# Inverse square roots as one GpSimd power, and filling products ahead of the first scores of an attention

## The chip, the cores and the metric

One NeuronCore of a Trainium2 chip runs the whole program. The metric is the device time of one execution in microseconds (us), as the median of several runs. The core's engines are TensorE (PE, with PEld for its weight loads), VectorE (DVE), ScalarE (ACT), GpSimd (POOL) and SyncE (SP, which only issues DMAs). Each engine works through its own instructions in order; semaphores make one wait for another.

## The reference

The program is a two-layer encoder over 512 tokens of width 1024. The first layer has two attentions side by side, A (grouped queries, normalised per head) and B (through latents), the second layer a neighbourhood attention; each layer ends in an MLP, and a last norm closes. What matters here is where an inverse square root is taken: in every RMS norm, of tokens, of heads and of latents.

```python
def rmsnorm(x, g):
    xf = x.astype(jnp.float32)
    y = xf * lax.rsqrt(jnp.mean(xf * xf, axis=-1, keepdims=True) + EPS)
    return (y * g.astype(jnp.float32)).astype(x.dtype)
...
    z = h @ w_in
    qa, ka, va, cq, ckv, kr = jnp.split(z, EVEN_SPLITS, axis=-1)
    qa = axial_rope(rmsnorm(qa.reshape(b, s, A_HEADS, HEAD_DIM), a_q_norm), row, col)
    ka = axial_rope(rmsnorm(ka.reshape(b, s, A_KV_HEADS, HEAD_DIM), a_k_norm), row, col)
    va = va.reshape(b, s, A_KV_HEADS, HEAD_DIM)
    oa = block_attention(qa, ka, va, HEAD_DIM ** -0.5)
    qb = (rmsnorm(cq, b_q_norm) @ b_w_uq).reshape(b, s, B_HEADS, B_NOPE + B_ROPE)
    ...
    kvb = (rmsnorm(ckv, b_kv_norm) @ b_w_ukv).reshape(b, s, B_HEADS, B_NOPE + B_V)
```

## The kernel before

**Precision.** Matrix products run on values split into a high and a low part (`hi`, `lo`): the high part is a rounded copy made by ACT, the low part the difference made by DVE or POOL. A product of two split operands is three matmuls (L501 to L503 for the dense ones).

**The first layer's beginning.** The input x is transposed to feature-major tiles, and the first 768 columns of the input projection (one key tile, one value tile, four query tiles of A) are accumulated in six PSUM banks. While the last products run, the banks are emptied one after the other. First comes the token norm: `compact_r` (L522, L524) sums the squares and makes `r0`, [128, 4], through `rsqrt`, and L764 and L765 copy and square it. Then the key tile: `stat` squares it and reduces per head by matmuls (L593 ACT, L594 DVE, L595 POOL, L596 and L597 PE), `stats_to_tok` turns the result token-major (L572 ACT, L575 PE), scales it by `r0sq` (L578), adds epsilon (L580) and takes the root `rsA`, [128, 8] (L582). L661 spreads it, PE's L530 transposes it back, L665 multiplies the rotated key, and L669 and L670 split it. After that the four query tiles pass through the same `stat`, and `q_scales` makes their root `rsQ`, [128, 32], and from it `scA` (L710). `rope_q(0)` rotates the first query tile (L560 DVE, L562 POOL, L563 and L566 DVE) and splits it (L623 ACT, L624 DVE); the three other tiles come later, through DMAs (`far`).

**The attention.** `attend` (L961) walks over 64 steps: 32 for A (8 heads of four 128-query blocks), then 32 for B. A step makes its scores (L997, two matmuls of 512 columns in A, three in B) into one of two score banks `s`; DVE's L1001 scales them, takes the extreme and moves them out of the bank, in A with `scA` as the scale; ACT's L1003 takes the exponential; DVE's L1004 and POOL's L1005 normalise. Three steps later PE transposes the probabilities (L972, four matmuls), ACT and DVE split them (L974, L975), and every second step the value products follow (L985, eight matmuls); after four steps a head is folded (L946 ACT, L949 DVE).

**The fillers.** Between these, `step` calls `fill.run(1.5)`: it takes products from a queue for as many microseconds as a credit says, each product with a nominal price (`MM3`, 0.69 for three matmuls). In the queue are the rest of the input projection (L501 to L503, split by ACT's L212 and DVE's or POOL's L202), the rotary key, the latents (whose norm takes the root `rsB`, [128, 8]) and B's first projections of queries, keys and values (L907 to L909 for the values); from step 35 on, the output projection and the second half of B's projections. `heads_B` empties the queue before it begins.

**The order.** Here nothing is fixed by hand: the code gives the order in which the operations are written, and a scheduler moves instructions of one engine past each other where data allow. So neither the written place of `rsqrt` nor that of the fillers is the place that they get. Only in the second layer's attention is the written order kept (`fixed_order`).

**The root.** `rsqrt` is used seven times: for r0, rsA, rsQ and rsB in the first layer, once in each MLP (L1136 broadcasts it), and for the second attention's tokens (L1313). `rsqrt_steps` (L155) makes a first guess from the bits of the number (L159, L160), halves and negates the number (L162), and does three Newton steps of three operations (L166, L167, L169): twelve DVE instructions on a tile of 4, 8 or 32 columns. `soon` would put a step off where the order is fixed by hand; `rsqrt` is not called there.

Of the kernel before, what the change touches and what calls it, by code (L numbers as in the profile page):

```python
# [8 lines left out]
F32 = mybir.dt.float32  # L9
F32R = mybir.dt.float32r  # L10
I32 = mybir.dt.int32
AF = mybir.ActivationFunctionType
ALU = mybir.AluOpType
# [5 lines left out]
P = 128  # L19
# [11 lines left out]
def f32(ap):  # L31
    return ap.bitcast(F32)
# [3 lines left out]
def encoder_kernel(ctx: ExitStack, tc: tile.TileContext, ins, out, dbg=None):  # L36
    nc = tc.nc
    PE, ACT, DVE, POOL, SP = nc.tensor, nc.scalar, nc.vector, nc.gpsimd, nc.sync
# [22 lines left out]
    def nm(s):  # L61
        cnt[0] += 1
        return f"{s}_{cnt[0]}"
# [18 lines left out]
    def sbk():  # L82
        return bank("s", 2)

    def stb():
        return bank("t", 2)

    def ob():
        return bank("o", 1)
# [4 lines left out]
    def tiny(n, dt=F32):  # L94
        return tp.tile([P, n], dt, tag=f"ti{n}", name=nm("ti"))

    def keep(shape, dt, name):
        return big.tile(shape, dt, tag=name, name=name)
# [8 lines left out]
    POOL.memset(ones, 1.0)  # L107
    zeros = keep([P, 1], F32, "zeros")
    POOL.memset(zeros, 0.0)
    gs = Slot(F32)  # L110
    ACT.dma_start(cst, ins["cst"][:, 0:C_ROPE])
    ACT.dma_start(gs.t[0:16, 0:P], ins["norm_mix"].rearrange("l (k p) -> (l k) p", p=P))
# [42 lines left out]
    def rsqrt_steps(v, n, then):  # L155

        y = tiny(n)
        yi = y.bitcast(I32)
        DVE.tensor_scalar(yi, v.bitcast(I32), 1, None, op0=ALU.logical_shift_right)  # L159
        DVE.tensor_scalar(yi, yi, -1, 0x5F3759DF, op0=ALU.mult, op1=ALU.add)  # L160
        hv = tiny(n)
        DVE.tensor_scalar(hv, v, -0.5, 1.0, op0=ALU.mult, op1=ALU.mult)  # L162

        def newton(y, left):
            a = tiny(n)
            DVE.tensor_tensor(a, y, y, op=ALU.mult)  # L166
            DVE.tensor_tensor(a, a, hv, op=ALU.mult)  # L167
            y2 = tiny(n)
            DVE.scalar_tensor_tensor(y2, a, 1.5, y, op0=ALU.add, op1=ALU.mult)  # L169
            if left:  # L170
                soon(lambda: newton(y2, left - 1))
            else:
                then(y2)

        newton(y, 2)

    def rsqrt(v, n):
        got = []
        rsqrt_steps(v, n, got.append)
        return got[0]  # L180
# [83 lines left out]
    def soon(z, later=None):  # L264
        if fixed[0]:
            (off_d if later is None else later).append(z)
        else:
            z()
# [202 lines left out]
    class Fill:  # L471
# [8 lines left out]
        def step(self):  # L480
            try:
                self.credit -= next(self.q[0][1])
            except StopIteration:
                self.q.pop(0)
# [13 lines left out]
    fill = Fill()  # L498
# [442 lines left out]
    def fold(o, e):  # L941

        if e == 0:
            hold["pair"] = scratch()
        a, c, pair = 64 * e, scratch(), hold["pair"]
        ACT.activation(c[0:64, :], o[64:128, :], AF.Copy)  # L946

        def add():
            DVE.tensor_tensor(pair[a : a + 64, :], o[0:64, :], c[0:64, :], op=ALU.add)  # L949
            if e:  # L950
                O.append(Slot())
                soon_a(lambda o=O[-1]: split(pair, o.pair()))

        soon(add)
# [6 lines left out]
    def attend(heads, step):  # L961


        late_t, late_v = [], []

        def transpose(h, i, p):
            if i % 2 == 0:
                h["pt"] = Slot(), Slot()
            h3, l3 = (s_.t.rearrange("p (k q) -> p k q", k=4)[:, :, (i % 2) * P : (i % 2 + 1) * P] for s_ in h["pt"])
            tb = stb()  # L970
            for k in range(4):
                PE.transpose(tb[:, k * P : (k + 1) * P], p[:, k * P : (k + 1) * P], ident)  # L972
            t3 = tb.rearrange("p (k q) -> p k q", k=4)
            ACT.activation(h3, t3, AF.Copy)  # L974
            DVE.tensor_tensor(l3, t3, f32(h3), op=ALU.subtract)  # L975
            if i % 2:
                late_v.append((h, i // 2, h["pt"]))

        def values(h, half, pt):
            if half == 0:  # L980
                h["o"] = ob()
            o = h["o"]
            for k in range(4):
                for n, m in enumerate(pt):
                    PE.matmul(o[:, 256 * half : 256 * half + 256], h["vlhs"](k), m.t[:, 256 * k : 256 * k + 256],  # L985
                              start=k == 0 and n == 0, stop=k == 3 and n == 1, skip_group_check=True)
            for s_ in pt:
                s_.free()
            if half:
                fold(o, h["e"])  # L990
                h["after"]()

        def scores(h, i):
            s = sbk()
            pl = h["passes"](i)
            for n, (lh, rh) in enumerate(pl):
                PE.matmul(s, lh, rh, start=n == 0, stop=n == len(pl) - 1)  # L997
            h["done"](i)
            t = tiny(4)
            p = pp.tile([P, 512], F32, tag="p", name=nm("p"))  # L1000
            DVE.tensor_tensor_reduce(p, s, zeros.to_broadcast([P, S]), op0=ALU.add, op1=ALU.min, scale=h["scale"](i),  # L1001
                                     scalar=3e38, accum_out=t[:, 1:2])
            ACT.activation(p, p, AF.Exp, bias=t[:, 1:2], scale=-1.0, accum_out=t[:, 2:3])  # L1003
            DVE.reciprocal(t[:, 3:4], t[:, 2:3])  # L1004
            POOL.tensor_scalar(p, p, t[:, 3:4], 1.0, op0=ALU.mult, op1=ALU.mult)  # L1005
            return p

        for h in heads:
            for i in range(4):
                ripe = list(late_v)  # L1010
                p = scores(h, i)
                if len(late_t) == 3:
                    transpose(*late_t.pop(0))
                late_t.append((h, i, p))
                if ripe:
                    values(*late_v.pop(0))
                step(h, i)
        for x in late_t:
            transpose(*x)
            while late_v:  # L1020
                values(*late_v.pop(0))
            fill.run(1.5)

    def heads_A():
        for h in range(8):
            t, e, kv = h // 2, h % 2, h // 4
            if e == 0 and t < 3:
                rope_q(t + 1)
            q, k = QA[t].pair(), KA[kv].pair()

            def done(i, t=t, e=e):
                if e == 1 and t < 3 and i == 0:
                    sum_q(t + 1)
                if i == 3 and e:
                    QA[t].free()
                    if t % 2:
                        KA[t // 2].free()

            yield dict(e=e, done=done, scale=lambda i, h=h: hold["scA"][:, i, h : h + 1],
                       passes=lambda i, q=q, k=k, e=e: [(q[:, e, i * P : (i + 1) * P], k[:, z, :]) for z in range(2)],  # L1040
                       vlhs=lambda kt, kv=kv: VAv[:, kt, kv, :], after=VA.free if h == 7 else lambda: None)

    def heads_B(g):
        fill.until(f"v{g}")
        Q, K, V = (QKV[g][z] for z in "QKV")
        vv = [s_.t.rearrange("p (i h e) -> p i h e", i=2, h=4) for s_ in V]
        for j in range(4):
            q, k = Q[j].pair(), K[j].pair()

            def passes(i, q=q, k=k):  # L1050
                ts = slice(i * P, (i + 1) * P)
                return [(q[0:96, 0, ts], k[0:96, 0, :]), (q[0:96, 1, ts], k[0:96, 0, :]),
                        (q[0:96, 0, ts], k[0:96, 1, :])]

            def done(i, j=j):
                if i == 3:
                    Q[j].free()
                    K[j].free()

            def after(j=j):  # L1060
                if j == 3:
                    for s_ in V:
                        s_.free()

            yield dict(e=j % 2, done=done, after=after, scale=lambda i: hold["scB"][:, i : i + 1], passes=passes,
                       vlhs=lambda kt, j=j: vv[kt // 2][:, kt % 2, j, :])
# [3 lines left out]
    def all_heads():  # L1070
        yield from heads_A()
        yield from heads_B(0)
        yield from heads_B(1)
# [18 lines left out]
    fill.add("z", rotary_key())  # L1092
    fill.add("z", latents())
    projB(0, False)
    attend(all_heads(), step)
    fill.until("out")
    ok = [s_.pair() for s_ in O[4:]]
# [631 lines left out]
```

## Time and profile before

| | us |
|---|---|
| median of three runs | 1184.7 |
| the three runs | 1183.35, 1184.7, 1185.4 |
| profiled execution: span from the first to the last instruction | 1184.0 |
| PE busy in it | 1160.5 (98%) |
| DVE busy in it | 883.2 (75%) |
| ACT busy in it | 640.3 (54%) |
| POOL busy in it | 526.1 (44%) |

The time of a run is the device's; the span of the profiled execution lies 0.7 us under the median of the runs. Busy time counts instructions that do work. A PE that is busy all the time need not be at its peak: matmuls overlap, so the distance between the starts of two says more than their durations. In the timeline a row gives start, duration, engine, line, operation, the tile written and the tiles read, their shapes and the number of merged instructions; the bracket at the end is the idle time of the engine before the row, with the instruction that ended it. In the groups of instructions the columns are busy time in all and mean duration in ns, then idle time before them and who ended it.

### The profile page before, as it was taken

The page shows a single profiled execution, that of the slowest core. Times are in us where ns is not written, and L with a number is a line of the kernel's source. Part 1 is how long each engine was busy: PE and PEld are TensorE (multiplying, and loading weights), DVE is VectorE, ACT ScalarE, POOL GpSimd, SP SyncE. Part 2 cuts the span into 40 slices and gives each one's busy share as a digit, 9 for nine tenths or more (in the row PEclk, how much of TensorE's full clock was granted, in tenths as well). Part 3 has the DMA queues.
Part 4 walks back from the last instruction along what each step waited for, and adds up shares of the span by engine and source line. Part 5 has one row for each costly group of instructions (what it writes and reads, how often), then busy time and mean ns, then how long its engine had stood idle before and what let it go on. Part 6 is the DMA issues. An engine that isn't in the chain of part 4 may idle for free.

```text
span 1184.0 us, 19784 instructions
## 1 busy us (share of the span) xinstructions
PE 1160.5 (98%) x7128; PEld 1021.2 (86%) x7128; DVE 883.2 (75%) x1514; ACT 640.3 (54%) x1081; POOL 526.1 (44%) x662
## 2 busy tenths in 40 slices
PE   9989999999999999999999999999999999999997
PEld 8667778888899899988998998988889989998895
DVE  5788998878967368786884676667996736778975
ACT  4468676664546247562553565555554624666344
POOL 3267343224562377819602232231376625774710
PEclk9999999999999999999999999999999999999998
DMA  7223225212524723225226464433352341322412
GB/s 244 71 54 92 68 78 134 62 56 77 167 86 134 263 70 90 72 90 165 67 72 178 131 184 126 116 112 109 107 165 76 115 134 55 98 64 89 143 36 71
DMA packets 110145, 128.01 MB, mean 108 GB/s; under 512 B 9075, under 2 KB 86816, under 8 KB 110048
## 3 DMA queue, kind: packets, MB, share of 16 engines
q1 hardware_dynamic: 106992, 119.30, 33.5%
q0 software_dynamic: 2304, 6.31, 2.2%
q8 instruction: 56, 0.92, 0.3%
q10 hardware_dynamic: 752, 1.15, 0.3%
q14 instruction: 41, 0.34, 0.1%
HBM read 104.32 MB, written 6.29 MB: 93 GB/s over the span
## 4 chain that ended last, share of the span: by engine, by line
PE 81%; DVE 4%; ACT 1%; issue 1%; POOL 0%; DVEq 0%; ACTq 0%
PE mm L503 8%; PE mm L501 8%; PE mm L502 8%; PE mm L390 4%; PE mm L389 4%; PE mm L388 4%; PE t L388 3%; PE t L389 3%; PE t L390 3%; PE s L502 2%; PE s L503 2%; PE s L501 2%; PE s L390 2%; PE s L388 2%; PE s L389 2%; PE s L997 2%
## 5 line engine op out<-in xcount | busy, mean ns | idle before, releaser
L309 DVE TENSOR_TENSOR wlo<-a,whi 128x896 fp32r<-128x896 f32 x132 | 161.8, 1230 | 83.7 <-ACT whi L308 82.9
L308 ACT ACTIVATE whi<-a 128x896 fp32r<-128x896 f32 x132 | 125.0, 950 | 155.0 <-PE o L502 45.8
L501 PE MATMUL mm<-a,whi 128*128 128x512 f32 x485 | 195.9, 406 | 0.9 <-DVE a L915 0.7
L503 PE MATMUL mm<-a,wlo 128*128 128x512 f32 x485 | 192.1, 397 | 2.5 <-DVE wlo L202 2.5
L502 PE MATMUL mm<-a,whi 128*128 128x512 f32 x485 | 192.5, 397 | 0.1
L202 DVE TENSOR_TENSOR wlo<-raw,whi 128x1024 fp32r<-128x1024 f32 (+4 forms) x117 | 139.3, 1193 | 66.4 <-ACT whi L212 63.9
L212 ACT ACTIVATE whi<-raw 128x1024 fp32r<-128x1024 f32 (+3 forms) x120 | 116.4, 971 | 92.2 <-PE s L502 39.8
L302 POOL TENSOR_TENSOR a<-a 128x128 f32<-128x128 f32 x132 | 85.1, 645 | 173.3 <-DMA a<-in_ffn_w_up_dram 103.9
L303 POOL TENSOR_TENSOR a<-a 128x256 f32<-128x256 f32 x132 | 120.2, 910 | 10.3
L304 POOL TENSOR_TENSOR a<-a 128x128 f32<-128x128 f32 x132 | 115.1, 872 | 10.3
L503 PEld LDWEIGHTS mm<-a,wlo 128*128 128x128 f32 x485 | 91.7, 189 | 23.7 <-DVE wlo L202 3.4
L501 PEld LDWEIGHTS mm<-a,whi 128*128 128x128 f32 x485 | 91.8, 189 | 20.4 <-PE t L972 0.9
L502 PEld LDWEIGHTS mm<-a,whi 128*128 128x128 f32 x485 | 91.9, 190 | 17.4 <-DVE a L545 0.4
L388 PE MATMUL mm<-a,whi 128*128 128x256 f32 x370 | 103.9, 281 | 0.0
L389 PE MATMUL mm<-a,whi 128*128 128x256 f32 x370 | 103.9, 281 | 0.0
L390 PE MATMUL mm<-a,wlo 128*128 128x256 f32 x370 | 103.7, 280 | 0.0
L1005 POOL TENSOR_SCALAR p<-p,ti 128x512 f32<-128x512 f32 x64 | 46.2, 724 | 92.3 <-DVE ti L1004 81.1
L1430 POOL TENSOR_SCALAR p<-p,ti 128x256 f32<-128x256 f32 x64 | 35.6, 567 | 104.8 <-DVE ti L1429 91.8
L388 PE MATMUL t<-a,whi 128*128 128x256 f32 x264 | 74.2, 281 | 0.0
L389 PE MATMUL t<-a,whi 128*128 128x256 f32 x264 | 74.1, 281 | 0.0
L390 PE MATMUL t<-a,wlo 128*128 128x256 f32 x264 | 73.9, 280 | 0.0
L390 PEld LDWEIGHTS mm<-a,wlo 128*128 128x128 f32 x370 | 69.6, 188 | 0.2 <-DVE wlo L309 0.2
(338 smaller groups left out, 3210.8 us busy)
## 6 DMA issues: line engine op xcount, KB each, us to landing
a<-in_ffn_w_up_dram SPq DMA_DIRECT2D x104, 256.0 KB
raw<-in_ffn_w_down_dram SPq DMA_DIRECT2D x46, 512.0 KB
raw<-in_od_w_qkv_dram SPq DMA_DIRECT2D x64, 128.0 KB
a<-in_ffn_w_down_dram SPq DMA_DIRECT2D x28, 256.0 KB
raw<-in_ffn_w_up_dram SPq DMA_DIRECT2D x12, 512.0 KB
raw<-in_ev_w_in_dram SPq DMA_DIRECT2D x12, 384.0 KB
a<-a SPq DMA_DIRECT2D x18, 256.0 KB
bias<-bx SPq DMA_DIRECT2D x16, 256.0 KB
```

Of the source, the lines that this page charges most:

```text
L202: z = lambda: (eng or DVE).tensor_tensor(to, src, f32(high), op=ALU.subtract)
L212: ACT.activation(hi[:, 0:m], raw[:, 0:m], AF.Copy)
L303: POOL.tensor_tensor(r[:, 4:6], r[:, 2:3].to_broadcast([P, 2, P]), r[:, 0:7:6], op=ALU.add)
L304: POOL.tensor_tensor(r[:, 7], r[:, 3], r[:, 5], op=ALU.subtract)
L308: ACT.activation(hi[:, 0:896], raw[:, 128:1024], AF.Copy)
L309: DVE.tensor_tensor(lo[:, 0:896], raw[:, 128:1024], f32(hi[:, 0:896]), op=ALU.subtract)
L388: PE.matmul(o, wh, x[:, 0], start=kp == 0 and n in (0, 1, 3, 5), stop=False, skip_group_check=True)
L389: PE.matmul(o, wh, x[:, 1], start=False, stop=False, skip_group_check=True)
L390: PE.matmul(o, wl, x[:, 0], start=False, stop=kp == self.np - 1, skip_group_check=True)
L501: PE.matmul(o, wh, xh, start=first, stop=False)
L502: PE.matmul(o, wh, xl, start=False, stop=False)
L503: PE.matmul(o, wl, xh, start=False, stop=last)
```

## The change

Two things are changed. `rsqrt_steps` becomes one GpSimd instruction, a power with the exponent -0.5 that is read from a constant column, for all seven roots. And in front of the call of `attend` stands `fill.run(5.5)`, so that the filling queue starts with a credit of 5.5 us.

```diff
@@ -107,6 +107,8 @@
     POOL.memset(ones, 1.0)
     zeros = keep([P, 1], F32, "zeros")
     POOL.memset(zeros, 0.0)
+    half = keep([P, 1], F32, "half")
+    POOL.memset(half, -0.5)
     gs = Slot(F32)
@@ -155,24 +157,8 @@
     def rsqrt_steps(v, n, then):
 
         y = tiny(n)
-        yi = y.bitcast(I32)
-        DVE.tensor_scalar(yi, v.bitcast(I32), 1, None, op0=ALU.logical_shift_right)
-        DVE.tensor_scalar(yi, yi, -1, 0x5F3759DF, op0=ALU.mult, op1=ALU.add)
-        hv = tiny(n)
-        DVE.tensor_scalar(hv, v, -0.5, 1.0, op0=ALU.mult, op1=ALU.mult)
-
-        def newton(y, left):
-            a = tiny(n)
-            DVE.tensor_tensor(a, y, y, op=ALU.mult)
-            DVE.tensor_tensor(a, a, hv, op=ALU.mult)
-            y2 = tiny(n)
-            DVE.scalar_tensor_tensor(y2, a, 1.5, y, op0=ALU.add, op1=ALU.mult)
-            if left:
-                soon(lambda: newton(y2, left - 1))
-            else:
-                then(y2)
-
-        newton(y, 2)
+        POOL.tensor_tensor(y, v, half.to_broadcast([P, n]), op=ALU.pow)
+        then(y)
@@ -1092,6 +1078,7 @@
     fill.add("z", rotary_key())
     fill.add("z", latents())
     projB(0, False)
+    fill.run(5.5)
     attend(all_heads(), step)
     fill.until("out")
```

DVE has 84 instructions fewer and POOL eight more (seven powers and a memset). The scheduler then orders all engines of the first layer anew; the lines of the changed kernel are 14 lower than the old ones between the root and the call of `attend`, and 13 lower behind it.

On DVE, at the key's root: `rsA` is the statistic and its root, `ti` the small tiles of the Newton steps, `wlo` the low part of a filler's weights. Before:

```order
L578 TENSOR_TENSOR rsA<-t_444,r0sq 128x8
L580 TENSOR_SCALAR rsA<-rsA 128x8
L159 TENSOR_SCALAR ti_452<-rsA 128x8
L162 TENSOR_SCALAR ti_455<-rsA 128x8
L160 TENSOR_SCALAR ti_452<-ti_452 128x8
L202 TENSOR_TENSOR wlo_663<-raw_648,whi_662 128x768
L166 TENSOR_TENSOR ti_457<-ti_452 128x8
L202 TENSOR_TENSOR wlo_667<-raw_650,whi_666 128x768
L167 TENSOR_TENSOR ti_457<-ti_457,ti_455 128x8
L169 SCALAR_TENSOR_TENSOR ti_460<-ti_457,ti_452 128x8
```

In the changed kernel, where L564, L566, L568, L647 and L651 are the old L578, L580, L582, L661 and L665:

```order
L564 TENSOR_TENSOR rsA<-t_428,r0sq 128x8
L552 TENSOR_TENSOR sc_441<-sc_441,sc_439 128x512
L566 TENSOR_SCALAR rsA<-rsA 128x8
L568 TENSOR_TENSOR rsA<-ti_436,r_129 128x8
L647 COPY sc_446<-rsA 128x512
L188 TENSOR_TENSOR wlo_589<-raw_574,whi_588 128x768
L651 TENSOR_TENSOR sc_452<-sc_441,t_445 128x512
L188 TENSOR_TENSOR wlo_593<-raw_576,whi_592 128x768
```

The two weight splits, which stood among the Newton steps, now stand behind the root, and L568 follows L566 with nothing between them but the wait for POOL.

On DVE, at the queries' root and the first query split (L610 is the old L624, L987 the old L1001). Before, the two splits stood among the Newton steps, ahead of the last six of them; now:

```order
L564 TENSOR_TENSOR rsQ<-t_544,r0sq 128x32
L549 TENSOR_TENSOR sc_558<-sc_558,a_134 128x512
L566 TENSOR_SCALAR rsQ<-rsQ 128x32
L552 TENSOR_TENSOR sc_560<-sc_560,sc_558 128x512
L568 TENSOR_TENSOR rsQ<-ti_552,r_129 128x32
L696 TENSOR_SCALAR scA<-rsQ 128x32
L610 TENSOR_TENSOR a_557<-sc_560,a_557 64x512 x2
L987 ISA p_643,ti_642<-s_639,zeros,scA 128x512
```

Both splits stand behind the root and `scA` now. On POOL, the power of `rsQ` stands behind both multiplications L562 of the rotations and ahead of the first low part of a filler's weights.

On PE, around the first scores (L997 before, L983 now; `s` is a score bank, `mm` a bank of the fillers). Before:

```order
L997 MATMUL s_634<-a_129,a_609 128x512 x2
L997 MATMUL s_679<-a_129,a_609 128x512 x2
L502 MATMUL mm_643<-a_121,whi_708 128x512
L503 MATMUL mm_643<-a_121,wlo_709 128x512
L501 MATMUL mm_644<-a_120,whi_708 128x512
L502 MATMUL mm_644<-a_120,whi_708 128x512
L503 MATMUL mm_644<-a_120,wlo_709 128x512
L501 MATMUL mm_644<-a_121,whi_708 128x512
L502 MATMUL mm_644<-a_121,whi_708 128x512
L503 MATMUL mm_644<-a_121,wlo_709 128x512
L501 MATMUL mm_645<-a_120,whi_708 128x512
L997 MATMUL s_694<-a_129,a_609 128x512 x2
```

Now:

```order
L489 MATMUL mm_571<-a_120,wlo_593 128x512
L983 MATMUL s_639<-a_131,a_557 128x512 x2
L983 MATMUL s_657<-a_131,a_557 128x512 x2
L487 MATMUL mm_569<-a_121,whi_592 128x512
L488 MATMUL mm_569<-a_121,whi_592 128x512
L489 MATMUL mm_569<-a_121,wlo_593 128x512
L983 MATMUL s_678<-a_131,a_557 128x512 x2
L487 MATMUL mm_570<-a_121,whi_592 128x512
L983 MATMUL s_693<-a_131,a_557 128x512 x2
```

Between the second scores and the third stood nine filling matmuls, and stand three. Between the token norm's sums (L522, now L508) and the first scores stood 76 matmuls of 512 columns from the projection and the fillers, and stand 63. In attention steps 1 to 24 the order has 114 such matmuls where it had 77, in steps 25 to 37 it has 6 where it had 39, and in step 38 15 where it had 6. From step 39 on the two orders are nearly the same.

## The prediction

> **What bounds the kernel now.** I read the table of stretches first, then the timeline of the first 170 us engine by engine, then the groups of instructions. Seven stretches around the place of the change (columns: stretch and length; busy time and count of PE, PEld, DVE, ACT, POOL; granted clock; DMA share; GB/s):
>
> ```profile
> span 1184.0 us, 19784 instructions
> 46.20:63.30 17.10, 14.40 (x61) 8.99 (x59) 13.47 (x37) 10.01 (x20) 6.48 (x5) 1.00 0.25 63
> 63.30:69.00 5.70, 4.34 (x22) 3.29 (x21) 5.12 (x11) 2.40 (x4) 4.80 (x4) 1.00 0.28 58
> 69.00:73.80 4.80, 3.22 (x13) 2.31 (x13) 4.35 (x11) 2.46 (x3) 2.30 (x2) 1.00 0.47 162
> 73.80:79.00 5.20, 4.39 (x12) 3.45 (x13) 3.59 (x10) 3.15 (x8) 0.69 (x1) 0.67 0.00 0
> 79.00:132.90 53.90, 51.76 (x293) 39.53 (x293) 46.45 (x121) 40.43 (x89) 35.20 (x38) 1.00 0.28 73
> 132.90:157.50 24.60, 23.16 (x151) 19.93 (x150) 23.83 (x56) 21.55 (x46) 7.22 (x10) 1.00 0.36 82
> 157.50:170.10 12.60, 12.60 (x78) 10.76 (x77) 11.16 (x28) 9.28 (x22) 7.01 (x9) 1.00 0.29 81
> ```
>
> PE is the bound: it works nearly all the time, and length less PE busy gives its idle time, 2.70, 1.36, 1.58, 0.81, 2.14, 1.44 and 0 us, 10.0 us in these 124 us. In the stretch from 73.8 the granted clock is 0.67, so 0.33 x 5.2 = 1.7 us more are lost. About 11.7 us is thus all that can be won here. DVE is the second bound: from 132.9 to 157.5 it is busy 23.83 of 24.60 us. So the question is which wait of PE goes and where DVE then makes PE wait instead.
>
> **The chain to the first key.** The inverse roots r0 (n=4) and rsA (n=8) stand in one chain: statistic, r0, rsA, broadcast.
>
> ```profile
> 41.59 0.16 DVE L524 TENSOR_SCALAR ti<-t 128x4 f32<-128x4 f32 x1 [1.00 <-PE t L522]
> 46.75 0.17 DVE L764 COPY r<-ti 128x4 f32<-128x4 f32 x1
> 51.56 0.43 DVE L661 COPY sc<-rsA 128x512 f32<-128x512 f32 x1
> 52.05 0.66 PE L530 MATMUL t<-cst,sc 128*128 128x128 f32 x4 [0.52 <-DVE sc L661]
> 53.35 0.42 DVE L594 CAST sc<-sc 128x512 fp32r<-128x512 f32 x1
> 40.67 1.27 POOL L595 TENSOR_TENSOR sc<-sc,sc 128x512 fp32r<-128x512 f32 x1 [8.92 <-DVE sc L594]
> 42.36 1.29 POOL L562 TENSOR_TENSOR sc<-sc,a 128x512 f32<-128x512 f32 x1 [0.42 <-PE s L502]
> ```
>
> From the end of L524 (41.75) to the end of L661 (51.99) are 10.2 us, most of them Newton steps. The change takes 12 tiny DVE operations out at each root and puts one GpSimd power in. No row shows a power, so its price has to be bounded:
>
> ```profile
> 12.45 1.52 POOL L517 TENSOR_TENSOR acc<-acc,sc 128x512 f32<-128x512 f32 x1 [6.63 <-ACT sc L515]
> 559.85 0.46 POOL L302 TENSOR_TENSOR a<-a 128x128 f32<-128x128 f32 x1
> ```
>
> An undisturbed two-input pass takes 0.46 us for 128 columns and 1.29 us (L562 above) for 512: 0.83/384 = 2.16 ns a column and 0.18 us to start. Lower end: a power costs one pass, 0.19, 0.20 and 0.25 us for n = 4, 8 and 32. Upper end: 24 separate passes (twice the Newton's twelve), 24 x that, 4.5, 4.7 and 6.0 us. I take 24 passes inside one instruction, because start-up is paid once per instruction in all these rows: 0.18 + 24 x 0.00216 n, that is 0.39, 0.59 and 1.84 us. It is an estimate, nearer the lower end. Below nothing it cannot be: the same instruction's start is in every row.
>
> After: 41.75 + 0.1 to reach POOL (its L595 ends at 41.94) + 0.39 gives 42.4; r0 and its square 0.4, L560 and L563 (held by POOL's L562, as the 1.29 us stand), rsA's two small operations and L566 bring 45.2; the power 0.7 with its hops 45.9; L582 and L661 46.55. That is 5.4 us earlier. PE reaches the transposes behind it (L530), moved up by 20 products, at about 46.2 and waits 0.4, as it waited 0.52. DVE has two weight splits and L665 to do before the first L594, so that one comes at 49.0, 4.3 us earlier. The query statistics behind it are a relay of ACT, DVE, POOL and PE; I let the relay keep its spacing, so its last link, PE's L575, moves from 63.3 to 59.0.
>
> **The chain to the first scores.**
>
> ```profile
> 63.30 0.41 PE L575 MATMUL t<-cst,sc 8*128 8x8 f32 x4
> 61.94 3.75 POOL L562 TENSOR_TENSOR sc<-a,a 128x512 f32<-128x512 f32 x2
> 68.22 0.68 DVE L624 TENSOR_TENSOR a<-sc,a 64x512 fp32r<-64x512 f32 x1
> 68.95 1.20 PE L997 MATMUL s<-a,a 128*128 128x512 f32 x4 [1.36 <-DVE a L624]
> 73.46 0.18 DVE L710 TENSOR_SCALAR scA<-rsQ 128x32 f32<-128x32 f32 x1
> 73.80 0.75 DVE L1001 CUSTOM_DVE_ANT_0 p<-s,zeros,scA 128x512 f32<-128x512 f32 x1 [0.15 <-DVE scA L710]
> 74.61 0.76 PE L997 MATMUL s<-a,a 128*128 128x512 f32 x2 [2.39 <-DVE ti L1001]
> ```
>
> There are two waits here: 1.36 us for the query's low half (L624), and then 2.39 us, because both score banks are full until scA lets L1001 read the first. Behind the second wait comes the half clock. Now the power of rsQ waits on POOL until L562 ends (2.4 us after L575), takes 1.84, and DVE's L582, L710 and then L624 stand behind it in order: 2.4 + 0.1 + 1.84 + 0.45 + 0.68 = 5.5 us after L575, so the first scores start at 64.5, 4.45 earlier. scA exists before them, so the second wait goes, and I expect the half clock to go with it: the wait left in front of the first scores is 5.5 less the 16 products and four transposes that stand there (4.0), 1.5 us, shorter than the 2.39 us after which the clock fell. The Trainium skill, TensorE: Matmul & The Clock Gate, Part 1, puts the fall to half rate after an idle window of about 3.4 us, by which 1.5 us is safe too; the trace differs from it, for here a shorter wait was enough.
>
> The fillers that `fill.run(5.5)` brings are not extra work. Counted in the order, 76 products of 512 columns stand between L522 and the first scores before, and 63 now, although 5.5 us are asked for: the roots are quicker, so less fits in front. The rest follows the scores.
>
> **From the first scores to the 39th.** From the 39th scores on both orders agree almost row for row, so the gain or loss is read there. PE's rates:
>
> ```profile
> 107.74 0.62 PE L997 MATMUL s<-a,a 128*128 128x512 f32 x2
> 108.20 0.60 PE L972 MATMUL t<-cst,p 128*128 128x128 f32 x4
> 108.56 1.19 PE L985 MATMUL o<-a,a 128*128 128x256 f32 x8
> 109.59 0.39 PE L501 MATMUL mm<-a,whi 128*128 128x512 f32 x1
> 128.87 0.63 PE L997 MATMUL s<-a,a 128*128 128x512 f32 x2
> 147.98 0.28 PE L908 MATMUL mm<-wlo,a 128*128 128x256 f32 x1
> 148.10 0.28 PE L909 MATMUL mm<-whi,a 128*128 128x256 f32 x1
> ```
>
> By the starts, a score product of 512 columns takes 0.23 us (a filler the same), four transposes 0.36, a value product 0.129, a short one 0.12. Row 128.87 is the 25th scores. Up to these the change has 37 fillers, 20 transposes, 13 value products, 19 short ones and one broadcast more: 8.5 + 1.8 + 1.7 + 2.3 + 0.4 = 14.7 us. Before took 128.87 - 68.95 = 59.9 us; less 2.39 and 1.7, plus 14.7, is 70.5, and the other 2.14 us of idle stay in it. The 25th scores start at 135.0.
>
> Then the queue of fillers is empty until attention step 35 adds more. In steps 25 to 37 the order has only 6 fillers against 39, and DVE decides:
>
> ```profile
> L975 DVE TENSOR_TENSOR a<-t,a 128x512 fp32r<-128x512 f32 x17 | 11.6, 685 | 0.8 <-ACT a L974 0.8
> L830 DVE TENSOR_TENSOR a<-sc,a 128x512 fp32r<-128x512 f32 x5 | 3.6, 738 | 0.0
> L949 DVE TENSOR_TENSOR sc<-o,sc 64x512 f32<-64x512 f32 x4 | 2.7, 684 | 0.1
> L1004 DVE RECIPROCAL ti<-ti 128x1 f32<-128x1 f32 x15 | 2.4, 159 | 0.6 <-ACT p L1003 0.5
> L202 DVE TENSOR_TENSOR wlo<-raw,whi 128x768 fp32r<-128x768 f32 x2 | 2.1, 1057 | 0.0
> L915 DVE SCALAR_TENSOR_TENSOR a<-mm,rsB,a 128x256 fp32r<-128x256 f32 x4 | 1.9, 475 | 0.0
> 167.58 0.73 DVE L1001 CUSTOM_DVE_ANT_0 p<-s,zeros,scB 128x512 f32<-128x512 f32 x1
> 170.10 0.75 DVE L1001 CUSTOM_DVE_ANT_0 p<-s,zeros,scB 128x512 f32<-128x512 f32 x1 [0.74 <-PE s L997]
> ```
>
> These steps hold 13 L1001 (0.67 to the next start), 12 L975, 12 L1004, 3 L949, 3 L830, 4 L915 and 2 L202: 8.7 + 8.2 + 1.9 + 2.1 + 2.2 + 1.9 + 2.1 = 27.1 us, and 26 allowing for the 0.07 us by which neighbours overlap. PE has 31 score, 44 transposing, 43 value, 6 filling and 5 short products there, 18.6 us, so it waits some 7 us: that is the price of the fillers spent early. The 25th L1001 comes 0.6 after its scores, at 135.6; the 38th (167.58 before) at 161.6. Step 38 then takes 15 delayed fillers, transposes, values and scores, 3.45 + 0.36 + 1.03 + 0.7 = 5.5 us, against 2.5. The 39th L1001 starts at 167.1, against 170.1: **3.0 us won.**
>
> The other four roots I cost at nothing. rsB falls inside the stretch, between scores. Those of the two MLPs and of the second attention have products of the same matrix on PE while they are made, and POOL has finished its weight sums; without that cover each would be worth one power. What follows step 39 is the same rows three us earlier, weights and loads with them.
>
> The sum is made against the profiled execution, whose span of 1184.0 us lies 0.7 under the median of 1184.7; taking 3.0 from the median gives 1181.7.
>
> **Rivals.** *The tail takes it all back.* If the 24 regular steps cost PE 0.13 us of waiting each beyond the 2.14 us kept, 3 us go and the time is 1184.7. For it: DVE is already full in 132.9 to 157.5 and now gets keys and values earlier. Against it: Newton steps leave DVE, and from 157.5 to 170.1 PE had no idle time in steps of the same pattern.
>
> *The power is slow.* Three of them stand in series before the first scores, and DVE waits in order behind each: L764, then L582, then L582 again, with the key, the query halves and every L1001 queued behind them. In the forecast the three cost 2.8 us; every further microsecond is paid once, and from 5.8 us on nothing is left. At the upper end they cost 15.2; the middle of 5.8 to 15.2 is 10.5, with the half clock back (1.7): 4.7 + 1.7 slower than now, 1191.1. For it: no arithmetic beyond single passes has been seen on POOL. Against it: four to 32 columns are little work at 2 ns a column.
>
> *The first power is dear, the others not:* paid once, at r0, where PE waits at the transposes L530 for every microsecond over the forecast. The first add (12.45) took 1.52 us against 1.29 later, 0.23 more; so much gives 1181.9, and from 3.0 us on it would undo the gain. The Trainium skill, GPSIMD Engine Reference, 2.1 Instruction dispatch, gives about 6 us, with no instruction of its own in the profile, for the first call of a freshly loaded routine; by it the sum would be about 1189 (an estimate). The first add does not bear it out.
>
> *The change does more than this:* the 2.14 us and the waits of the steps go too and the power costs one pass. That wins 2.2 + 2.1 + some 2 of the tail more, 1175.4.
>
> **How the numbers follow.** The forecast has 0.50, at 1181.7 with a range of its own of 1179 to 1184. The more favourable case has 0.08, the tail 0.14, the slow power 0.24, the dear first power 0.04. About 0.2%, 2.4 us, is what a measurement can tell from none. Of the forecast's 0.50 I put 0.41 above that and 0.09 below; with the 0.08, faster has 0.49. Of the tail's 0.14, 0.10 lie within and 0.04 beyond on the slow side: same 0.19, slower 0.04 + 0.24 + 0.04 = 0.32. The range runs from near the favourable case's end to the slow power's middle, 1176 to 1191.
>
> **What would show it.** Right: the seven powers under 2 us; first scores near 64.5, with no second wait and no 0.67 clock behind them; PE idle in steps 25 to 37, some 7 us; the 39th L1001 near 167. Wrong: a power of several us with L582 waiting on POOL; a half clock in 46 to 80; or PE idle in the first 24 steps.

## The result, and the profile after

The changed kernel takes 1189.04 us (median of five runs, 1187.94 to 1190.96), the kernel before beside it 1184.76 us (five runs, 1183.35 to 1185.84): a ratio of 1.0041, 95% interval 1.0029 to 1.0054. It is slower by 4.3 us, where 3 us faster was forecast. The profiled execution took 1188.34 us, with a span of 1186.6.

The first view is that of one line, the power, in the changed kernel (duration in ns as smallest, median, largest, then the first and the last start):

```profile
L160 POOL TENSOR_TENSOR ti<-ti,half x4: 1017/1032/1045, 41.6 to 844.7; 128x4 f32<-128x4 f32 x4
L160 POOL TENSOR_TENSOR ti<-rsA,half x1: 1638/1638/1638, 46.5 to 46.5; 128x8 f32<-128x8 f32 x1
L160 POOL TENSOR_TENSOR ti<-rsQ,half x1: 5791/5791/5791, 63.9 to 63.9; 128x32 f32<-128x32 f32 x1
```

The price grows with the columns, and much faster than was taken: 5.79 us for 32 columns against 1.84. Three of them stand in series before the first scores, r0's (41.64 in the timeline below), rsA's and rsQ's: 1.04 + 1.64 + 5.79 = 8.47 us, where the forecast had 2.82 and put the point of no gain at 5.8.

What stands behind the wide one is seen in the timeline of the changed kernel, rows of three engines:

```profile
41.33 0.16 DVE L510 TENSOR_SCALAR ti<-t 128x4 f32<-128x4 f32 x1 [1.00 <-PE t L508]
41.64 1.04 POOL L160 TENSOR_TENSOR ti<-ti,half 128x4 f32<-128x4 f32 x1
...
61.35 0.41 PE L561 MATMUL t<-cst,sc 8*128 8x8 f32 x4
63.86 5.79 POOL L160 TENSOR_TENSOR ti<-rsQ,half 128x32 f32<-128x32 f32 x1
69.62 1.26 POOL L188 TENSOR_TENSOR wlo<-raw,whi 128x512 fp32r<-128x512 f32 x1
69.69 1.24 DVE L568 TENSOR_TENSOR rsQ<-ti,r 128x32 f32<-128x32 f32 x1 [5.31 <-POOL ti L160]
70.84 1.25 POOL L549 TENSOR_TENSOR sc<-sc,a 128x512 f32<-128x512 f32 x1
70.96 1.17 DVE L696 TENSOR_SCALAR scA<-rsQ 128x32 f32<-128x32 f32 x1
72.16 1.41 DVE L610 TENSOR_TENSOR a<-sc,a 64x512 fp32r<-64x512 f32 x2
72.90 2.08 PE L983 MATMUL s<-a,a 128*128 128x512 f32 x4 [7.28 <-DVE a L610]
174.66 0.75 DVE L987 CUSTOM_DVE_ANT_0 p<-s,zeros,scB 128x512 f32<-128x512 f32 x1 [0.75 <-POOL wlo L188]
```

DVE waits 5.31 us for the power. Then two operations on 32 columns (0.18 us for L710 before) take 1.24 and 1.17 us while POOL's next two passes (L188 and L549) run, and only then come the two low halves (L610). The first scores start when the first of them is done, halfway through the 1.41 us. PE stands still for 7.28 us ahead of the first scores, and these run at a half clock: four products take 2.08 us, against 1.20 before. The 39th score reduction (old L1001, now L987) is at 174.66.

The same stretches as before, in the changed kernel:

```profile
46.20:63.30 17.10, 12.69 (x58) 8.53 (x59) 12.49 (x23) 9.60 (x19) 10.54 (x7) 1.00 0.29 69
63.30:69.00 5.70, 2.33 (x11) 1.57 (x9) 1.08 (x2) 3.18 (x4) 5.58 (x2) 0.89 0.28 72
69.00:73.80 4.80, 0.90 (x2) 0.80 (x3) 3.79 (x4) 0.00 (x0) 3.10 (x3) 0.50 0.27 82
73.80:79.00 5.20, 5.20 (x15) 4.05 (x15) 2.97 (x9) 2.44 (x6) 0.00 (x0) 0.60 0.00 0
79.00:132.90 53.90, 53.01 (x299) 42.21 (x298) 42.17 (x103) 40.56 (x88) 36.46 (x40) 1.00 0.26 72
132.90:157.50 24.60, 23.84 (x144) 18.87 (x143) 23.99 (x57) 20.49 (x45) 5.93 (x10) 1.00 0.41 92
```

Length less PE busy is now 4.41, 3.37, 3.90, 0, 0.89 and 0.76 us: 4.3 us more idle time than before between 63.3 and 73.8, 1.7 more in the stretch ahead, 0.8 less from 73.8 to 79 and 1.9 less in the two long ones. The clock of 0.60 from 73.8 to 79 takes 2.1 us (0.67 took 1.7 before), the 0.50 in the stretch ahead of it some 0.4 more.

### The profile page after: what moved, and what is told of

Its sections match the earlier page's. It is cut to its first block, busy times and chain, and to the rows that moved or that the text cites. A ratio compares the mean times of both kernels' runs of the same rounds, so it can differ in the third digit from the quotient of the medians.

```text
span 1186.6 us, 19691 instructions
## 1 busy us (share of the span) xinstructions
PE 1158.4 (98%) x7128; PEld 1020.3 (86%) x7128; DVE 868.8 (73%) x1430; ACT 640.1 (54%) x1081; POOL 539.1 (45%) x670
## 4 chain that ended last, share of the span: by engine, by line
PE 84%; DVE 6%; issue 4%; POOL 2%; ACT 2%; DMA 0%; SPq 0%; DVEq 0%; ACTq 0%; POOLq 0%
PE mm L487 8%; PE mm L489 8%; PE mm L488 8%; PE mm L376 3%; PE mm L375 3%; PE mm L374 3%; PE s L487 3%; PE s L489 3%; PE s L488 3%; PE s L983 2%; PE t L375 2%; PE t L374 2%; PE t L376 2%; PE o L971 2%; PE s L376 2%
## 5 line engine op out<-in xcount | busy, mean ns | idle before, releaser
L188 DVE TENSOR_TENSOR wlo<-raw,whi 128x1024 fp32r<-128x1024 f32 (+4 forms) x117 | 139.0, 1190 | 69.6 <-ACT whi L198 69.4
L288 POOL TENSOR_TENSOR a<-a 128x128 f32<-128x128 f32 x132 | 87.5, 662 | 173.3 <-DMA a<-in_ffn_w_up_dram 106.5
L290 POOL TENSOR_TENSOR a<-a 128x128 f32<-128x128 f32 x132 | 117.4, 889 | 10.3
L376 PE MATMUL t<-a,wlo 128*128 128x256 f32 x264 | 73.8, 279 | 0.0
```

Source lines behind the costliest of these rows:

```text
L188: z = lambda: (eng or DVE).tensor_tensor(to, src, f32(high), op=ALU.subtract)
L290: POOL.tensor_tensor(r[:, 7], r[:, 3], r[:, 5], op=ALU.subtract)
L376: PE.matmul(o, wl, x[:, 0], start=False, stop=kp == self.np - 1, skip_group_check=True)
```

## The experiments

T1 is the theory that the price of the 32-wide power, which stands alone on the path to the first scores, makes the loss. T2 says that the fillers taken early do it, T3 that the narrow powers in the key's chain do. T4 came later: a long power on GpSimd costs wherever it stands.

### One part at a time

A switch says which roots are a power; the others take the twelve Newton steps. The kernels differ in it and in the credit. The edit is against the kernel before; its last line stands only in the kernels with the credit.

```diff
+    POWER = lambda n: ...
     def rsqrt_steps(v, n, then):
+        if POWER(n):
+            y = tiny(n)
+            POOL.tensor_tensor(y, v, half.to_broadcast([P, n]), op=ALU.pow)
+            return then(y)
...
+    fill.run(5.5)
```

Narrow powers, Newton steps at 32 columns, with the credit:

> The 32-wide root goes back to twelve Newton steps on VectorE, the six narrower roots stay GpSimd powers and the credit of 5.5 us stays. T1, the 32-wide power of 5.79 us sets the first scores: TensorE's wait of 7.28 us before its first scores falls below 3 us, most of the half clock between 63 and 79 us goes, and the time comes to about 1184.5 us (1182.5 to 1186), since the short powers still cost the 1.7 us more idle time seen between 46.2 and 63.3 us while the later stretches keep the 1.9 us that they gained. T2, the fillers taken early make the loss: no change from the changed kernel, 1188 or more. T3, the narrow powers in the key's chain make it: 1187 or more.

All powers, no credit:

> All seven roots are powers, the credit of 5.5 us is taken out. T1 (the wide power): the wait before the first scores stays near 7.3 us, because as many products stand in front of the first scores without the credit (117) as with it; 1189 us (1187.5 to 1191). T2 (the early fillers): back to 1184.8 (1183 to 1186). T3 (the narrow powers): as T1.

Newton steps everywhere, with the credit:

> All seven roots by Newton as before, only the credit of 5.5 us is put in. T1 and T3: 1184.8 us within 1.2, no wait over 3 us before the first scores. T2 (the early fillers): about 1189.

The wide power alone, no credit:

> Only the 32-wide root is a power, the six others are Newton steps, no credit. T1: the power of 5.8 us is there, with the query's low half behind it, and TensorE waits 5 us or more before its first scores; 1188 us (1186.5 to 1190.5). T2 and T3: 1184.8 within 1.2.

And narrow powers, Newton steps at 32 columns, no credit:

> The 32-wide root by Newton steps, the other six by powers, no credit: the kernel with Newton steps at the wide root, without its credit. If the credit is worth nothing either way: 1183.4 us within 1. If it costs (T2 in a smaller size): below 1182.4. If it pays: above 1184.4.

| kernel | wide power | narrow powers | credit | median us | ratio to before, 95% interval |
|---|---|---|---|---|---|
| changed kernel | yes | yes | yes | 1189.04 | 1.0041 [1.0029, 1.0054] |
| all powers, no credit | yes | yes | no | 1190.08 | 1.0051 [1.0039, 1.0063] |
| wide power alone | yes | no | no | 1190.97 | 1.0053 [1.0041, 1.0065] |
| narrow powers and credit | no | yes | yes | 1183.39 | 0.9994 [0.9986, 1.0003] |
| narrow powers alone | no | yes | no | 1183.65 | 0.9997 [0.9988, 1.0006] |
| credit alone | no | no | yes | 1184.89 | 1.0006 [0.9996, 1.0016] |

The three kernels with the wide power are 0.4 to 0.5% slower than before, the three without it can't be told from before. Taken in pairs, the wide power costs 5.7 us beside narrow powers and credit (1189.04 against 1183.39), 6.4 beside narrow powers (1190.08 against 1183.65) and 6.5 alone (1190.97 against the 1184.43 of the kernel before in the same series), near its own length. T1 holds; T2 and T3 fall. Only one median lies outside its band: the wide power alone took 0.5 us more than its upper end. In its timeline the power takes 5.46 us and PE waits 8.58:

```profile
66.95 5.46 POOL L162 TENSOR_TENSOR ti<-rsQ,half 128x32 f32<-128x32 f32 x1
75.68 2.08 PE L1005 MATMUL s<-a,a 128*128 128x512 f32 x4 [8.58 <-DVE a L632]
```

Without the wide power (narrow powers and credit), the timeline reads there:

```profile
66.94 1.20 PE L1005 MATMUL s<-a,a 128*128 128x512 f32 x4 [1.36 <-DVE a L632]
70.59 0.74 PE L1005 MATMUL s<-a,a 128*128 128x512 f32 x2 [0.40 <-DVE ti L1009]
167.58 0.75 DVE L1009 CUSTOM_DVE_ANT_0 p<-s,zeros,scB 128x512 f32<-128x512 f32 x1 [0.74 <-POOL wlo L210]
```

So the second wait, 2.39 us before, is down to 0.40 when the root comes earlier, as was forecast, and the time still does not fall. That question is taken up below.

### The dose

```diff
-        POOL.tensor_tensor(y, v, half.to_broadcast([P, n]), op=ALU.pow)
+        for _ in range(2 if n == 32 else 1):
+            POOL.tensor_tensor(y, v, half.to_broadcast([P, n]), op=ALU.pow)
```

> As the changed kernel, but the 32-wide power is made twice, the same result written twice by GpSimd. T1: every microsecond of the power is paid once, so 5.8 us more than the changed kernel: 1194.8 us (1194 to 1196.5), the wait before the first scores 13 us. If the loss came from the new order of the instructions instead of the duration, the time would stay within 2 us of 1189.

Measured: 1194.84 us, ratio 1.0088 [1.0075, 1.0101], 5.8 us more than the changed kernel. Its timeline:

```profile
63.84 11.29 POOL L161 TENSOR_TENSOR ti<-rsQ,half 128x32 f32<-128x32 f32 x2
78.39 2.07 PE L984 MATMUL s<-a,a 128*128 128x512 f32 x4 [12.76 <-DVE a L611]
```

The power is 5.50 us longer, PE's wait 5.48, the program 5.8: every microsecond of it is paid, and nothing hides any part.

### The queue behind the waiting instruction

The rotation of the first query tile is written ahead of the scales, and the multiplication that waits for the power is put behind the two low halves on DVE:

```diff
-    q_scales()
     rope_q(0)
+    q_scales()
...
-        DVE.tensor_tensor(v3, y..., op=ALU.mult)
+        last = lambda: DVE.tensor_tensor(v3, y..., op=ALU.mult)
+        if n == 8:
+            with tc.issue_after(hold["low"].ins):
+                last()
+        else:
+            last()
```

> All as in the changed kernel, but the rotation of the first query tile is written ahead of the scales, and VectorE's two low halves of it are issued before the instruction that waits for the 32-wide power. T1: the power is still 5.8 us and ends at about the same time, but TensorE gets its first two pairs of scores done and waits behind them, at the third, for some 4 us; the two low halves (1.4 us) and 1.2 us of score products leave the path, so 1186.5 us (1185 to 1188). If the queue behind the waiting instruction were the whole loss, the time would be 1184.5 or less; if it were nothing, 1189.

Measured: 1187.97 us, ratio 1.0032 [1.0020, 1.0044]. In its timeline the wait has moved, as T1 says, to the third scores:

```profile
65.67 1.20 PE L988 MATMUL s<-a,a 128*128 128x512 f32 x4 [0.97 <-DVE a L615]
72.50 1.22 PE L988 MATMUL s<-a,a 128*128 128x512 f32 x2 [4.93 <-DVE ti L992]
```

The first scores come 7.2 us earlier than in the changed kernel, and with both banks full PE waits for `scA` instead. The order in the queue is worth about 1 us by the medians, but the two intervals overlap, so that this gain is not shown. Most of the loss stays while the order changes, and with it the power of 5.42 us.

### The power where nothing waits for it

The first head needs only its own four of the 32 columns. The root is taken in two, and DVE reads the second part behind the first four score reductions (L1017 here):

```diff
+        for a, b in ((0, 1), (1, 8)):
+            n = b - a
+            v = keep([P, 4 * n], F32, "rsQ%d" % a)
...
+            y = rsqrt(v, 4 * n)
...
+    def scale_A(h, i):
+        if h not in hold["scA"]:
+            with tc.issue_after(hold["red"].ins):
+                hold["rest"]()
+        return hold["scA"][h][:, i]
```

> All seven roots stay GpSimd powers and the credit stays, but the 32-wide root is taken in two: four columns for the first head, then 28 for the others, whose end VectorE reads only behind the first four score reductions. T1, the wide power is dear because VectorE and TensorE stand behind it before the first scores: by 0.35 us and 0.17 us a column the first part takes 1.03 us and the second 5.1 us, the first scores start near 67 us instead of 72.9, the half clock is gone and the time is about 1183 us (1181.5 to 1185). T4, a long power on GpSimd costs wherever it stands, because GpSimd's weight differences and normalisations queue behind it: 1187 or more.

Measured: 1183.8 us, ratio 0.9995 [0.9986, 1.0004]. Its timeline:

```profile
62.85 1.38 POOL L160 TENSOR_TENSOR ti<-rsQ,half 128x4 f32<-128x4 f32 x1
64.59 5.17 POOL L160 TENSOR_TENSOR ti<-rsQ,half 128x28 f32<-128x28 f32 x1 [0.36 <-DVE rsQ L706]
65.81 1.40 DVE L610 TENSOR_TENSOR a<-sc,a 64x512 fp32r<-64x512 f32 x2 [0.58 <-ACT a L609]
66.55 1.20 PE L1012 MATMUL s<-a,a 128*128 128x512 f32 x4 [1.19 <-DVE a L610]
167.63 0.75 DVE L1017 CUSTOM_DVE_ANT_0 p<-s,zeros,scB 128x512 f32<-128x512 f32 x1 [0.73 <-PE s L1012]
```

A power of 5.17 us runs beside the first scores and costs nothing that can be measured: T4 falls. (The power of four columns took 1.38 us here, where 1.03 was expected.) What it costs is decided by what stands behind it.

The next three change the split kernel or the one with Newton steps at 32 columns. In the first, the second part of 28 columns takes Newton steps, in the order that the scheduler gives them:

> As the split root, but the 28 columns of the other heads take Newton steps on VectorE; the first head's four columns and the five other roots are powers. T1: the first scores start near 67.5 us with no second wait, 1183.5 us (1182 to 1185). T4 (a long power costs wherever it stands) says the same here; the two differ by the other split kernel.

Measured: 1186.9 us (1183.72 to 1189.2), ratio 1.0017 [1.0006, 1.0028], outside the range that was given. In its trace the scheduler set the first six of the twelve steps ahead of and between the two low halves, and PE waits for its first scores:

```profile
69.19 1.20 PE L1020 MATMUL s<-a,a 128*128 128x512 f32 x4 [3.50 <-DVE a L632]
```

That does not explain the median, for this trace is of the fastest of the twelve executions: its granted clock is 1.00 from 63.3 to 79 us, behind the wait too. Over the whole program the mean granted clock is 0.995 to 0.998 in the five executions below 1186 us and 0.992 to 0.995 in the seven above. So the slower ones lose clock somewhere; that they lose it behind this wait is likely, but not shown. In the second, the narrow roots take Newton steps and the two powers stay:

> The queries' root in two powers, of 4 and of 28 columns, the second read behind the first four score reductions, as in the split kernel; the six narrower roots by Newton steps again; the credit stays. It asks whether the waits that are left (2.8 us at the key's transposes in the split kernel, 0.5 with Newton steps there) can be taken out too. If what TensorE idles less before the 39th scores is kept to the end: the second wait of 2.39 us and the half clock of 1.7 us are gone and the key's wait is short, 1181.5 us (1180 to 1183). If it is given back by the 39th scores or later, as the small gains of the split kernels let one think: 1184 us within 1.

Measured: 1184.6 us, ratio 1.0012 [1.0003, 1.0021]: what was won is given back, and a little more. PE waited 0.5 us at the key, but 2.52 at the first scores, with a clock of 0.64 from 69.0 to 73.8. In the third no power is left:

> No power at all: the queries' root in two, of 4 and of 28 columns, both by Newton steps, the second behind the first score reduction; all other roots by Newton steps; the credit stays. T1 holds that the power does nothing that Newton steps don't do as well when the wide part stands off the path to the first scores: within 1 us of the kernel with the two powers and Newton steps elsewhere, 1182 to 1184. If freeing VectorE of the twelve steps matters: 2 us or more slower than that.

Measured: 1190.49 us, ratio 1.0050 [1.0036, 1.0063]. My addition to T1, that Newton steps do as well there, was wrong. Rows of its timeline on three engines:

```profile
69.41 1.60 POOL L204 TENSOR_TENSOR wlo<-raw,whi 128x512 fp32r<-128x512 f32 x1 [2.89 <-ACT whi L214]
69.89 1.14 DVE L168 TENSOR_TENSOR ti<-ti 128x4 f32<-128x4 f32 x1
70.97 1.27 POOL L565 TENSOR_TENSOR sc<-sc,a 128x512 f32<-128x512 f32 x1
71.06 1.20 DVE L169 TENSOR_TENSOR ti<-ti,ti 128x4 f32<-128x4 f32 x1
72.30 0.16 DVE L171 SCALAR_TENSOR_TENSOR ti<-ti,ti 128x4 f32<-128x4 f32 x1
73.83 0.90 PE L1028 MATMUL s<-a,a 128*128 128x512 f32 x2 [2.24 <-DVE ti L1033]
83.85 0.73 PE L1028 MATMUL s<-a,a 128*128 128x512 f32 x2 [2.10 <-DVE ti L1033]
```

The twelve steps of the second part are issued behind the first score reduction here, where the split kernel reads its power behind the fourth. Two steps of the first part, 0.16 us each when alone (L171), take 1.14 and 1.20 us beside POOL's passes, and PE waits 2.24 us for the first reduction; twelve steps of the second part stand ahead of the second head's first reduction, and PE waits 2.10 us more. In the orders tried here, a long power off the path is better than twelve short steps on the engine that PE waits for.

### The wait at the key

The last kernel takes the one with Newton steps at 32 columns and puts the second half of the key's work two projections later, so that the wait at the key's transposes is covered. In the waits of the kernel that it starts from (total, times, longest) it is

```profile
PE t L538 <- DVE sc L669: 2.8, 1, 2.8
```


```diff
         krot = rope(kg, cosA, sinA, sw16)
+        hold["key"] = lambda: key_end(rs, krot)
+    def key_end(rs, krot):
         bk = stb()
...
             ev_q(m - 2, banks[m])
+        if m == 2:
+            hold["key"]()
```

> As the kernel with Newton steps at the 32-wide root, powers at the six others and the credit, but the second half of the key's work (spread, transposes, multiplication, split) is written two projections later, behind the first query tile's statistics, so that eleven more products stand ahead of the key's transposes on TensorE. If the 2.8 us that TensorE waits there is worth its length: the wait falls below 0.6 us and the time is 1181 us (1179.5 to 1182.4). If what is won so early is given back by DVE-bound steps or elsewhere: 1183.4 us within 1, as without the move.

Measured: 1184.18 us, ratio 0.9998 [0.9988, 1.0007]. In its waits, the one at the transposes fell to 0.4 us, and others took its place, at the query statistics:

```profile
PE t L605 <- POOL sc L603: 3.8, 3, 2.0
PE t L604 <- DVE sc L602: 1.3, 1, 1.3
PE t L538 <- DVE a L693: 0.4, 1, 0.4
```

The longest, 2.0 us, is for POOL's low part of a statistic (L603), which starts at 48.65 us, when the power of rsA (46.94, 1.74 us) leaves POOL. A power that is no longer waited for in one place is waited for in the next.

### How far one execution moves by itself

The kernels of narrow powers with Newton steps at 32 columns have their 39th reductions 2.5 us (with the credit) and 3.1 us (without) ahead of the 170.10 of before, and no better median. So both kernels were profiled once more, unchanged:

> The kernel before, unchanged, profiled once more. If the first trace was of a late execution: the first scores and the 39th score reduction stand up to 1.5 us earlier than 68.95 and 170.10 us, with a span of 1182 to 1183 us, and so the kernels without the wide power win 1 to 1.5 us by the 39th scores, not 2.5 to 3.1. If the marks repeat within 0.3 us, their gain is real there and is lost behind.

> The changed kernel, unchanged, profiled once more: the seven powers within 0.1 us of 1.03, 1.64 and 5.79 us, the wait before the first scores within 0.3 us of 7.28, the 39th score reduction within 1 us of 174.66.

The changed kernel repeated: 5.79 us for the power, 7.26 us for the wait, 173.81 for the 39th reduction, 1189.41 us. The kernel before did not. Rows of its second timeline (first products, second wait, 39th reduction), and then the stretch behind that wait:

```profile
1.00 4.40 PE L136 MATMUL o<-ones 128*128 128x128 f32 x22 [1.00 <-POOL zeros L109]
73.59 0.74 PE L997 MATMUL s<-a,a 128*128 128x512 f32 x2 [2.38 <-DVE ti L1001]
167.37 0.75 DVE L1001 CUSTOM_DVE_ANT_0 p<-s,zeros,scB 128x512 f32<-128x512 f32 x1 [0.73 <-PE s L997]
```

```profile
73.80:79.00 5.20, 5.20 (x26) 3.80 (x26) 4.44 (x16) 3.99 (x11) 2.17 (x4) 1.00 0.00 0
```

Its 39th reduction is 2.73 us earlier: 1.0 us from the program's first eight microseconds (the first 22 products took 5.06 us in the first trace), so that its first scores start at 67.94 instead of 68.95, and 1.7 us because the half clock is absent, behind a wait of the same length (2.38 against 2.39). Measured by this trace, the kernel with narrow powers and credit starts its scores 1.0 us earlier (66.94) and has its 39th reduction at 167.58, not earlier. The first trace was of a late execution: wherever both are on record for the kernel before, the time lies 2.0 to 2.2 us above the span, so a span of 1184.0 belongs to a time near 1186, above the median of 1184.7 and not 0.7 under it.

There is one more place where the clock differs from one execution to the next. At the last score reduction of the second attention the two traces of the changed kernel (811.12 and 810.40) are 7.3 and 6.6 us behind the second trace of before (803.85), as much as at the 39th. From there to the end they take 375.4 and 377.2 us, the two traces of before 377.7 and 377.9. In this stretch PE waits once, near 1100 us, for the low part of a weight (first the first trace of the changed kernel, then its second):

```profile
1106.89 0.50 PE L489 MATMUL mm<-a,wlo 128*128 128x512 f32 x1 [1.98 <-DVE wlo L188]
1106.40 0.50 PE L489 MATMUL mm<-a,wlo 128*128 128x512 f32 x1 [2.00 <-DVE wlo L188]
```

The kernel before waits 2.23 and 2.67 us there. In slices of 5 us the granted clock falls to 0.76 behind this wait in the second trace of the changed kernel, to 0.76 and 0.66 in the two of before, and stays at 1.00 in the first trace of the changed kernel. So the span of 1186.6 has some 1.8 us in its favour that the next execution of the same kernel did not have.

## Why the prediction was wrong

**What bounds the kernel** held: PE is busy 98% before and after, and the loss is idle time and half clock in the stretches named. That 1.7 us of half clock can be won did not hold: it is in one trace of before and not in the other.

**The price of the power is the step that failed.** It was taken as "24 passes inside one instruction", 0.39, 0.59 and 1.84 us, "nearer the lower end" between bounds of 0.25 and 6.0 for 32 columns. The runs show 1.03, 1.64 and 5.42 to 5.79: at 32 columns near the upper end, at 4 and 8 in the lower third of the bounds. From 4 to 32 columns it grows by (5.79 - 1.03) / 28 = 0.17 us a column, 79 times the 2.16 ns of a pass, where 24 passes were taken. The reason given, that few columns are little work, took the width of the tile for the work in an element; no row of the trace had an operation of this kind, and that should have moved the value to the middle of the bounds and more chance to the slow rival.

**The chain to the first key**: L661 was put at 46.55 and PE's wait at 0.4; the two powers took 2.68 us instead of 0.98, and PE waited 2.8 us at the transposes. The narrow kernels show that this wait costs nothing in the median, and the late key that covering it wins nothing.

**The chain to the first scores** was 5.5 us from L575 to scores at 64.5; they started at 72.90. The 8.4 us are L575 itself 2.35 late (61.35 against 59.0, the short powers among it), 0.1 ahead of the power, the power 3.95 longer, and 2.0 between its end and the scores (3.25 us from 69.65, against 1.23). These 2.0 are the two operations beside POOL's passes, L568 and L696: 1.24 + 1.17 us, where 0.45 was counted. The second wait did go, but into the first; the half clock came back in both traces of the changed kernel.

**From the first scores to the 39th** 102.6 us were forecast and 101.8 passed (72.90 to 174.66): the stretch was sized right, although half clock stood in it that the sum did not have. DVE was the bound in steps 25 to 37, as was forecast: between 145.0 and 171.5 it was busy 25.7 of 26.5 us, and the 25th and 38th reductions stand 26.6 us apart, where 26 were forecast. The 7 us of idle PE named as a sign do not appear: PE is shown as busy 25.9 of these 26.5 us.

**The slow power** was the rival with 0.24, and its rule was right where its price was open: "from 5.8 us on nothing is left". With the measured 8.47 it gives 8.47 - 5.8 = 2.7, with the half clock 1.7 more, 1189.1 us; 1189.04 was measured. That it comes so close is partly luck, since the 3 us of gain against which it counts were not there: the changed kernel's 39th reductions stand 6.4 to 7.3 us behind the second trace of before, and its medians 4.3 to 4.6. The delay lasts to the end of the second attention (7.3 and 6.6 us there) and is 4.8 and 5.8 us in the spans (1186.6 and 1187.6 against 1181.8); 1.8 us of it went in the first trace with the clock that did not fall near 1100 us. What brings the medians to 4.3 to 4.6 stays open.

**The tail** as a rival came true in its outcome, in the kernels of narrow powers with Newton steps at 32 columns: first scores 1 us earlier, and nothing or little left of it at the 39th (167.58 and 166.97 against 167.37). Its mechanism, PE waiting more, is not seen: with the credit PE's idle time up to 170 us is 10.0 us, against 11.0 in the second trace of before. What takes the gain stays open.

**The dear first power** did not show. The first power took 1.04 us like the later ones, and started 0.15 us after its input. The 6 us of the Trainium skill, GPSIMD Engine Reference, 2.1 Instruction dispatch, are not seen here. (Added to 1181.7 they make 1187.7, not the 1189 that was given.)

**The fillers and the other four roots**, costed at nothing, cost nothing: the kernels with the credit alone, and with the narrow powers alone, can't be told from before.

## What to carry to other kernels

An operation that no row shows has no price, and its width in columns says little: measure it alone, at each width, before it goes on a chain that the bounding engine waits for. A dear operation on an idle engine is free only if nothing in the queues of the busy engines stands behind its result; taking first the few columns that are needed first, and reading the rest later, made 5.2 us of it free here. And before a gain of 3 us is built on one trace, a second trace of the same kernel tells which of the waits and half clocks in it come every time.

## What the runs showed of the hardware

Whether a half clock follows a wait is not settled by the length of the wait: from 73.8 to 79 us the clock was 0.67 behind 2.39 us in one execution of the kernel before and 1.00 behind 2.38 in another; near 1100 us it fell behind 2.00 us and not behind 1.98 in two executions of the changed kernel; and behind the 3.50 us of the split kernel with Newton steps it stayed at 1.00. The Trainium skill, TensorE: Matmul & The Clock Gate, Part 1, has a free-running window of about 3.4 us, which would make it a matter of phase. The traces fit that, but do not show the window; that a wait shorter than it is sometimes enough, they add.

POOL's ordinary passes can hold DVE up: steps of 0.16 us took 1.14 and 1.20 beside passes of 1.60 and 1.27, and DVE's first two operations behind the wide power took 1.24 and 1.17 beside passes of 1.26 and 1.25. Each of the four ended within 0.05 us of the pass beside it. The Trainium skill, SBUF — State Buffer, section SBUF: two separate sides, calls the pair of ports of the two an exclusive lock, held for a whole instruction; for these passes the rows agree. Beside the power they do not: while the 5.17 us of 28 columns ran, DVE's two low halves, with two inputs each, took 1.40 us, as in the changed kernel, where the power had ended (1.41).
